# One transformer-like layer on one core: the order of every engine's instructions set by the kernel's own search instead of Tile's

## The chip, the cores and the metric

The kernel runs on one core of one Trainium2 chip. The metric is the device time of one execution in microseconds. Three executions of the kernel before took 917.09, 913.85 and 911.78 us; their median, 913.85 us, is the time before.

A core has a matrix engine (TensorE, PE in the profile, with its weight loads shown apart as PEld), a vector engine (VectorE, DVE), a scalar engine (ScalarE, ACT), GpSimd (POOL) and SyncE (SP), which issues most transfers. Each engine works through a list of instructions of its own in order, and waits on semaphores for the others. So the order of that list, which is fixed when the program is built, decides who waits for whom.

## What is computed

One layer of a hybrid backbone over 512 latent tokens and 256 context tokens with 1,024 channels, in float32. Cut to what matters:

```python
mod = silu(c) @ w_ada + b_ada                     # shifts, scales, gates
h, hc = rms_norm(x) * (1 + sc1) + sh1, rms_norm(ctx) * (1 + csc1) + csh1
aq, ak, av, dq, dk, dv, dz, da, db, ga, gd = split_cols(h @ w_in)   # the same for hc
y_attn = window_ctx_attention(q_a, k_a, v_a, k_ac, v_ac, attn_sink)
_, s_cf, s_cb = bidir_delta(context tokens, zero state)   # chunks of 64, both directions
o_dl, _, _ = bidir_delta(latent tokens, s_cf, s_cb)
y = sigmoid(ga) * (y_attn @ w_br_attn) + sigmoid(gd) * ((rms_norm(o_dl) * silu(dz)) @ w_br_dn)
x = x + gt1 * (y @ w_out)
x = x + gt2 * (square(relu((rms_norm(x) * (1 + sc2) + sh2) @ w_mlp1)) @ w_mlp2)
```

In the delta rule each chunk of 64 tokens needs the state that the chunk before it left:

```python
def step(S, xs):
    u = uv_c - w_c @ S
    o = qd_c @ S + intra_c @ u
    S = exp(gl_c) * S + k_tail_c.T @ u
```

There are 4 context chunks and 8 latent chunks in each direction. This is the serial part of the layer.

## The kernel before, in words

A matrix product in float32 is made of three products of float32r halves: weights and inputs are split into a rounded upper part (ScalarE copy) and the remainder (VectorE subtraction), and `mm3` (L293, L294, L295), `br_a` (L1086), `gate_tiles` (L1040) and `Pair.prod` (L1509) multiply upper by upper, upper by lower and lower by upper. `wload` brings a weight tile of 128x1024 into a ring of two raw buffers (`wr`), copies the upper part into one of three `wh` (L271) and makes the lower part in one of three `wl` (L276 on VectorE, or L273 on ScalarE and an accumulating transfer on GpSimd's queue, L274).

The stages, in the order in which the code is written and with the profile's times:

- 0 to 75 us: modulation vectors (`ada` L228, `columns` L244 to L258), the norm of x and ctx (L319 to L332), the modulated features (L299 to L301) and the first projections.
- 75 to 290 us: the other projections, queries and keys (`qk_norm` L451 to L465), the triangular matrices of the delta rule (`chunk_mats` L805 to L823) and their inversion on VectorE (`invert` L864, L865; transposes L841, L844, L875), attention (`scores` L545 to L582, `outputs` with its transposes L613 and products L602, L603). `weave` interleaves such pieces by hand.
- 290 to 393 us: the delta chain over the context chunks (`chain_step`: L1156 the products with the state, L1160 and L1161 on VectorE, L1175, L1181, L1187, L1195, L1206, L1213), the combination of the inverses (`combine` L885 to L909), the products within chunks (L786).
- 393 to 482 us: the chain over the latent chunks, both directions in turn, L1156 to L1223. Between its pieces `run_fill` puts matmuls of `br_a` and `gate_tiles` (L1040), which don't depend on the chain. `late_mod` (L1104, L1105) makes the remaining modulation vectors on VectorE, eight transfers and eight passes for each of four groups.
- 482 to 570 us: the norm of the chain's output (L1336), its transposes (L1341), the branch and output projections, the residual and the second norm.
- 570 us on: the MLP, one quarter with `mm3`, the others by a seven-product scheme (`Pair`, `combos`), and the products with the second MLP matrix (L1636 adds them).

SBUF is divided by the kernel itself: an arena hands out places when the code is traced, so that buffer addresses don't depend on the order of execution. What orders the instructions is Tile: the code is traced into one list, Tile finds the dependencies, and when the context ends, a scheduler with an estimate of each instruction's time lays out every engine's list, the earlier traced of those that it takes to be ready first. The kernel adds a few ties without semaphores: all functions of one activation table set stay behind its load (`act`, L154 to L168), and `follow` (L198) keeps one instruction behind another.

Of the kernel before, what the change touches and what calls it, by code (L numbers as in the profile page):

```python
# [2 lines left out]

# [14 lines left out]
NWR, NWS = 2, 3  # L18
# [13 lines left out]
FPAUSE, CPAUSE = 12, 12  # L32
NPL = ()
WEARLY = 0
ND1 = 3
NGD = 5
P = 128
# [8 lines left out]
HC = CH // 2  # L46
# [66 lines left out]
def tile_layer(ctx: ExitStack, tc: tile.TileContext, I: dict, out: bass.AP, dbg=None):  # L113
    nc = tc.nc
    V, A, G, PE = nc.vector, nc.scalar, nc.gpsimd, nc.tensor
# [17 lines left out]
    banks = Arena(lambda o, n: psum[:, o:o + n], 512, 8)  # L133
# [4 lines left out]
    alloc, bank = mem.get, lambda n=1: banks.get(n * 512)  # L138
# [13 lines left out]

    nosync = mybir.DependencyInfo(mybir.DependencyClass.NoSync, mybir.DependencyReason.DATA)
    actg = {"set": None, "head": None, "ops": []}  # L154

    def act(out_, in_, func, **kw):

        sets = TABLES.get(func)
        if sets and actg["set"] not in sets:
            head = A.preload_act_table_set(sets[0])  # L160
# [3 lines left out]
        r = A.activation(out_, in_, func, **kw)  # L164
        if sets:
            tc.add_manual_dep(r.ins, actg["head"].name, nosync, reason="table sets")
            actg["ops"].append(r.ins)
        return r  # L168

# [27 lines left out]

    def follow(later, earlier):  # L198

        tc.add_manual_dep(later.ins, earlier.ins.name, nosync, reason="order")  # L200

    def split(src, hi, lo, eng=None):
        A.activation(r32(hi), src, AF.Copy)  # L203
# [29 lines left out]
    last = [None]  # L233
# [159 lines left out]
    cost, sint = cs[:, :512], cs[:, 512:]  # L393
# [82 lines left out]
    own = [slice(0, 64), slice(64, 128)]  # L476
# [218 lines left out]
    t, t2 = alloc(TOK), alloc(TOK)  # L695
# [570 lines left out]
    for g in range(2):  # L1266
        ms = slice(16 * g, 16 * g + 16)
        f, b = xa[0][:, ms], xa[1][:, ms]
# [9 lines left out]
    for g in range(2):  # L1278
# [20 lines left out]
        for a in range(2):  # L1299
            lo, hi = quad(a, 0), quad(a, 1)  # L1300
# [37 lines left out]
    for qq in range(2):  # L1338
# [3 lines left out]
        for a in range(2):  # L1342
            n = 2 * qq + a
            t = alloc(512)
# [70 lines left out]
    ts = []  # L1415
# [13 lines left out]
    first = []  # L1429
# [5 lines left out]

    if WEARLY:
        load_first()
# [6 lines left out]
    for b in accs:  # L1444
        b.free()
    if not WEARLY:
        load_first()
# [139 lines left out]
    for hf in range(4):  # L1587
        act_, xs = [], []
        for f in range(0 if hf else FT):
            if first:  # L1590
                bufs, _, acc = first.pop(0)
            else:
                bufs = [alloc(1024), alloc(1024)]
                w = wload(I["wm1"][f], bufs=bufs)
                acc = bank()
                mm3(acc.ap.rearrange("p (n t) -> p n t", n=2), w, ms)
            r, hl = alloc(1024), alloc(1024)
            A.activation(r[:, :512], acc.ap, AF.Relu)
            acc.free()
            V.tensor_tensor(r[:, 512:], r[:, :512], r[:, :512], op=ALU.mult)  # L1600
            split(r[:, 512:], hl[:, :512], hl[:, 512:])
            for b in bufs + [r]:
                b.free()
            act_.append(hl)
            xs.append((r32(hl[:, :512]), r32(hl[:, 512:])))
            next(late)
        if hf == 0:
            xs7 = combos()
            for _ in late:
                pass  # L1610
            scr.free()
            for b in MH[0]:
                b.part(1024, 1024).free()
        w2 = lambda ct: wload(I["wm2"][ct * 4 + hf])
        ps_ = pairs[hf]
        for i, p_ in enumerate(ps_):
            p_.first()
            if i:
                p_.load2()
            if i + 1 < len(ps_):  # L1620
                p_.second()
            if i + 2 < len(ps_):
                ps_[i + 2].load1()
        ws = [w2(0), w2(1)]
        if hf:
            ps_[-1].second()
        accs = [bank(), bank()]
        ks = list(range(FT))
        for cols in (ks[:FT - 2], ks[FT - 2:]):
            for acc, w in zip(accs, ws):  # L1630
                mm3(acc.ap, w, [xs[k] for k in cols], start=(cols[0] == 0), stop=(cols[-1] == FT - 1), ks=cols)
        for ct in range(8):
            if ct > 1:
                accs.append(bank())
                mm3(accs[ct].ap, w2(ct), xs)
            V.scalar_tensor_tensor(xn_[ct], accs[ct].ap, modT[:, 3, ct:ct + 1], xn_[ct], op0=ALU.mult, op1=ALU.add)  # L1636
            accs[ct].free()
            if hf == 3:
                nc.sync.dma_start(out=out[ct], in_=xn_[ct])
            if hf < 3 and ct in (3, 5):  # L1640
                (pairs[hf + 1][0].load1 if ct == 3 else pairs[hf + 1][0].load2)()
        for b in act_:
            b.free()
        if hf < 3:
            pairs[hf + 1][1].load1()

# [109 lines left out]
```

## Time and profile before

| | |
|---|---|
| executions | 917.09, 913.85, 911.78 us |
| median | 913.85 us |
| span of the profiled execution, first to last instruction | 909.7 us |
| median less that span | 4.15 us |
| mean granted TensorE clock | 0.997 |
| bytes moved | 107.13 MB, 118 GB/s |

The profiled execution's time as a whole is not listed apart from its span; what lies around the span is part of the 4.15 us. In the rows below, a group's row has the line, the engine, the operation, output and inputs by name, the shapes and the count, then busy time and the mean of one in ns, then the idle time of the engine just ahead of these instructions and who ended it. A row of waits reads: who waited for whom, us in total, number of times, longest. A row of the timeline has start, duration, engine, line and operation. A row by stretch has start:end, length, and for PE, PEld, DVE, ACT and POOL the busy time and number of instructions, then the granted clock, the share of DMA time and GB/s. Matmul ends are modelled and overlap, so the distance between starts says more about TensorE than a matmul's duration: one 128x512 product of float32r starts 0.23 us after the one before it.

### The profile page before, as it was taken

Reading aid. Unit: us, or ns where it says so; the run is one execution under the profiler, and the core shown is the slowest. Engines: PE = TensorE matmul, PEld = TensorE weight load, DVE = VectorE, ACT = ScalarE, POOL = GpSimd, SP = SyncE. Lnnn points to the kernel's source line nnn. Section 1 sums busy time; section 2 is a strip of 40 time slices with the busy share of each in tenths; the row PEclk is TensorE's granted clock in tenths of the full one; section 3 lists DMA queues with packets and bytes.
Section 4 is the critical chain, followed back from the end, with each engine's and each line's share of the span. In section 5 each row is a group of like instructions: output and inputs, shape, how many; then the busy total and the mean of one; then the engine's idle time right before and its main releaser. Section 6 shows DMA issues by size and latency. Waiting matters only on the chain.

```text
span 909.7 us, 18033 instructions
## 1 busy us (share of the span) xinstructions
PE 873.9 (96%) x7564; PEld 721.3 (79%) x7564; DVE 652.9 (72%) x1111; ACT 496.9 (55%) x881; POOL 26.0 (3%) x42
## 2 busy tenths in 40 slices
PE   8999999989999998889999999999999999999998
PEld 6688667867777676656677789888898899889986
DVE  5665799876778999566666968896587567837631
ACT  6368764475768795475654434463265246424520
POOL 0000001010000001100000000000000000000000
PEclk9999999999999999999999999999999999999999
DMA  9824455532311136523143645453412332334031
GB/s 355 312 76 117 94 131 107 113 73 47 57 36 35 59 121 235 182 67 99 49 152 107 241 127 186 155 170 115 139 48 93 116 116 70 116 93 139 1 116 46
DMA packets 31985, 107.13 MB, mean 118 GB/s; under 512 B 4000, under 2 KB 4512, under 8 KB 31904
## 3 DMA queue, kind: packets, MB, share of 16 engines
q1 hardware_dynamic: 29600, 97.59, 32.1%
q0 software_dynamic: 2304, 8.39, 5.8%
q8 instruction: 59, 0.97, 0.4%
q14 instruction: 22, 0.18, 0.1%
HBM read 103.87 MB, written 2.10 MB: 116 GB/s over the span
## 4 chain that ended last, share of the span: by engine, by line
PE 60%; DVE 20%; ACT 11%; DMA 6%; issue 3%; SPq 0%; ACTq 0%; DVEq 0%
PE banks L293 12%; PE banks L294 12%; PE banks L295 12%; PE banks L1509 11%; PE banks L1040 5%; DMA m<-in_wada 3%; ACT m L164 2%; DVE m L865 2%; DVE m L864 2%; DVE m L1105 2%; DVE m L204 2%; DMA m<-in_wm 1%; DVE wl L276 1%; ACT m L928 1%; DVE m L875 1%
## 5 line engine op out<-in xcount | busy, mean ns | idle before, releaser
L293 PE MATMUL banks<-m,wh 128*128 128x512 f32 (+1 forms) x568 | 213.2, 376 | 0.5 <-ACT m L203 0.5
L294 PE MATMUL banks<-m,wh 128*128 128x512 f32 (+1 forms) x568 | 210.7, 371 | 0.3 <-DVE m L204 0.2
L295 PE MATMUL banks<-m,wl 128*128 128x512 f32 (+1 forms) x568 | 209.8, 370 | 0.0
L271 ACT ACTIVATE wh<-wr 128x1024 fp32r<-128x1024 f32 (+1 forms) x92 | 90.6, 987 | 130.5 <-PE banks L294 102.5
L1509 PE MATMUL banks<-m,m 128*128 128x256 f32 x1008 | 123.2, 284 | 0.9 <-ACT m L203 0.6
L1509 PEld LDWEIGHTS banks<-m,m 128*128 128x128 f32 x1008 | 121.9, 192 | 2.4 <-ACT m L203 1.2
L203 ACT ACTIVATE m<-m 128x512 fp32r<-128x512 f32 (+2 forms) x118 | 81.9, 719 | 75.0 <-DVE m L1487 12.0
L293 PEld LDWEIGHTS banks<-m,wh 128*128 128x128 f32 x568 | 107.0, 189 | 19.2 <-ACT m L203 1.0
L294 PEld LDWEIGHTS banks<-m,wh 128*128 128x128 f32 x568 | 107.0, 188 | 18.8 <-DVE m L204 1.2
L295 PEld LDWEIGHTS banks<-m,wl 128*128 128x128 f32 x568 | 106.9, 188 | 18.6 <-issue 0.7
L1040 PE MATMUL banks<-m,wh 128*128 128x512 f32 x320 | 108.2, 409 | 3.5 <-ACT m L164 3.5
L204 DVE TENSOR_TENSOR m<-m,m 128x512 fp32r<-128x512 f32 (+2 forms) x118 | 92.3, 804 | 22.3 <-ACT m L203 14.1
L276 DVE TENSOR_TENSOR wl<-wr,wh 128x1024 fp32r<-128x1024 f32 (+1 forms) x76 | 84.2, 1110 | 14.9 <-ACT wh L271 12.6
L1636 DVE SCALAR_TENSOR_TENSOR m<-banks,modT,m 128x512 f32<-128x512 f32 x32 | 24.0, 750 | 68.6 <-PE banks L295 68.4
L1040 PEld LDWEIGHTS banks<-m,wh 128*128 128x128 f32 x320 | 59.6, 190 | 16.5 <-ACT m L164 4.0
L1040 PE MATMUL banks<-m,wl 128*128 128x512 f32 x160 | 65.5, 410 | 0.0
L1105 DVE SCALAR_TENSOR_TENSOR m<-m,m 128x1024 f32<-128x1024 f32 x32 | 38.8, 1220 | 14.3 <-DMA m<-in_wada 14.2
L293 PE MATMUL banks<-m,m 128*128 128x256 f32 (+1 forms) x136 | 44.9, 344 | 1.4 <-ACT m L300 1.2
L294 PE MATMUL banks<-m,m 128*128 128x256 f32 (+1 forms) x136 | 45.1, 340 | 0.9 <-DVE m L301 0.8
L295 PE MATMUL banks<-m,m 128*128 128x256 f32 (+1 forms) x136 | 44.6, 337 | 0.0
L164 ACT ACTIVATE m<-banks,st 128x512 f32<-128x512 f32 (+1 forms) x32 | 23.5, 738 | 24.7 <-DVE st L570 24.4
L1040 PEld LDWEIGHTS banks<-m,wl 128*128 128x128 f32 x160 | 30.5, 190 | 6.5
(258 smaller groups left out, 1339.5 us busy)
## 6 DMA issues: line engine op xcount, KB each, us to landing
m<-in_wada SPq DMA_DIRECT2D x48, 512.0 KB, 5.3
wr<-in_wm SPq DMA_DIRECT2D x40, 512.0 KB, 3.6
wr<-in_win SPq DMA_DIRECT2D x39, 512.0 KB, 3.7
m<-in_wm SPq DMA_DIRECT2D x24, 512.0 KB, 3.9
wl<-in_win POOLq DMA_DIRECT2D x16, 512.0 KB, 5.6
m<-in_xT SPq DMA_DIRECT2D x8, 512.0 KB, 5.6
wr<-in_wbr SPq DMA_DIRECT2D x16, 256.0 KB, 2.6
wr<-in_wout SPq DMA_DIRECT2D x8, 512.0 KB, 3.8
```

What stands on the lines that cost most here:

```text
L164: r = A.activation(out_, in_, func, **kw)
L203: A.activation(r32(hi), src, AF.Copy)
L204: (eng or V).tensor_tensor(r32(lo), src, hi, op=ALU.subtract)
L271: upper[0] = A.activation(r32(hi), raw, AF.Copy)
L276: V.tensor_tensor(r32(lo), raw, hi, op=ALU.subtract)
L293: PE.matmul(acc, w[0][:, k, :], xhi, start=(start and i == 0), stop=False)
L294: PE.matmul(acc, w[0][:, k, :], xlo, start=False, stop=False)
L295: r = PE.matmul(acc, w[1][:, k, :], xhi, start=False, stop=(stop and i == n - 1))
L1040: PE.matmul(acc.ap, w[x][:, k, :], hx[k][y], start=(k == p == 0), stop=(k == KT - 1 and p == 2))
L1105: V.scalar_tensor_tensor(wa.ap, wa.ap, 0.5, scr.ap, op0=ALU.mult, op1=ALU.mult, accum_out=modT[:, grp, j:j + 1])
L1509: PE.matmul(dst, r32(self.w[w][i][:, k * P:(k + 1) * P]), xs7[x][k][j], start=(n == 0), stop=(n == 11))
L1636: V.scalar_tensor_tensor(xn_[ct], accs[ct].ap, modT[:, 3, ct:ct + 1], xn_[ct], op0=ALU.mult, op1=ALU.add)
```

## The change

The traced program stays the same; every instruction exists before and after with the same operands. `tie` records the kernel's own ordering ties. When tracing is done, `arrange` builds from the instructions a graph of its own (`needs`: reads and writes of cells of SBUF and banks of PSUM, rings of weight buffers, arena places that follow each other, the ties) and goes through it in time: of the instructions that are ready on the engine that is free first, the one traced first is taken, its occupancy and its end come from `Step.cost`, a transfer's end from a queue model, and what depends on it becomes ready `SIGNAL` = 120 ns later. Each engine's list is then tied in that order, so that Tile's scheduler has no choice left.

```diff
+SIGNAL = 120
...
+    ties = []
+
+    def tie(later, name):
+        tc.add_manual_dep(later, name, nosync, reason="order")
+        ties.append((later.name, name))
...
-                tc.add_manual_dep(head.ins, o.name, nosync, reason="table sets")
+                tie(head.ins, o.name)
...
-        tc.add_manual_dep(later.ins, earlier.ins.name, nosync, reason="order")
+        tie(later.ins, earlier.ins.name)
...
+    return ties
+
+
+class Step:
+
+    RINGS = {"wr": NWR, "wh": NWS, "wl": NWS, "st": 4}
...
+    def cost(self):
+
+        n = self.cols
+        if self.kind == "InstMatmult":
+            if self.dtype.endswith("32r"):
+                return max(60, 7 + .43 * n if n < 512 else 226), 300
+            if self.dtype.endswith("16"):
+                return 60, 200
+            if self.tile == (P, P):
+                return max(60, 110 if n <= P else 1.68 * n), 400
+            return (142 if self.tile[0] == P else 42 if self.tile[1] > HC else 20), 250
+        if self.kind == "InstStreamTranspose":
+            return 2010, 2100
+        if self.eng == "DVE":
+            own = 67 + 1.04 * n + 60 * self.psum if n > 8 else 100
+            return own, own + 85
+        if self.eng == "Activation":
+            own = 1290 if "Load" in self.kind else max(195, 36 + .893 * n) + 20 * self.psum
+            return own, own + 130
+        return 550, 560
+
+
+def needs(steps, ties):
...
+def arrange(tc, nc, ties):
+
+    steps = [Step(i) for i in nc.cur_bb.bb.instructions if "Boundary" not in type(i).__name__]
+    before = needs(steps, ties)
...
+    for _ in steps:
+        t, e = min((free[e] if here[e] else max(free[e], coming[e][0][0]), e) for e in engines if here[e] or coming[e])
+        while coming[e] and coming[e][0][0] <= t:
+            heapq.heappush(here[e], heapq.heappop(coming[e])[1])
+        k = heapq.heappop(here[e])
+        s = steps[k]
+        if "DMA" in s.kind:
+            rate, lag = (400., 1000) if e == "SP" else (159., 900)
+            links[e] = max(t + lag, links[e]) + s.bytes / rate
+            own, end = (350 if e == "SP" else 900), links[e] + 1300
+        else:
+            own, end = s.cost()
+            end += t
+        free[e] = t + own
+        own_ = "DMA" not in s.kind
+
+        def seen(n):
+            same = own_ and n < len(steps) and steps[n].eng == e
+            return free[e] if same and e == "PE" else end + 20 if same else end + SIGNAL
+
+        release(after[k], seen)
+        if e in last:
+            tc.add_manual_dep(s.ins, last[e], order, reason="order")
+        last[e] = s.name
...
-        tile_layer(tc, aps, out)
+        arrange(tc, nc, tile_layer(tc, aps, out))
```

More of the change, by code (lines that the diff above doesn't have):

```diff
@@ L1 @@
+import heapq
 import numpy as np
@@ L165, in act @@
         if sets:
-            tc.add_manual_dep(r.ins, actg["head"].name, nosync, reason="table sets")
+            tie(r.ins, actg["head"].name)
             actg["ops"].append(r.ins)
@@ new lines, in arrange, with release @@
+def arrange(tc, nc, ties):
+    steps = [Step(i) for i in nc.cur_bb.bb.instructions if "Boundary" not in type(i).__name__]
+    before = needs(steps, ties)
+    after, left, ready = [[] for _ in before], [len(b) for b in before], [0.] * len(before)
+    for k, b in enumerate(before):
+        for p in b:
+            after[p].append(k)
+    engines = {"PE", "DVE", "Activation", "Pool", "SP"}
+    free, links = dict.fromkeys(engines, 0.), {"SP": 0., "Pool": 0.}
+    coming, here, last = {e: [] for e in engines}, {e: [] for e in engines}, {}
+    def release(ns, at_):
+        for n in ns:
+            ready[n] = max(ready[n], at_(n))
+            left[n] -= 1
+            if not left[n]:
+                if n < len(steps):
+                    heapq.heappush(coming[steps[n].eng], (ready[n], n))
+                else:
+                    release(after[n], lambda _: ready[n])
+    first = [n for n, b in enumerate(before) if not b]
+    for n in first:
+        left[n] = 1
+    release(first, lambda _: 0.)
+    order = mybir.DependencyInfo(mybir.DependencyClass.NoSync, mybir.DependencyReason.DATA)
+    for _ in steps:
[8 more added lines that the diff above has]
+            own, end = (350 if e == "SP" else 900), links[e] + 1300
+        else:
+            own, end = s.cost()
[9 more added lines that the diff above has]
+        last[e] = s.name
```

76 lines of the change are left out of this document (added).

## The prediction

> **What bounds the kernel now.** I read the page's busy shares first, then the busy time by stretch, then who ends TensorE's idle time, then the timeline of the one stretch in which most of it lies.
>
> ```profile
> span 909.7 us, 18033 instructions
> ...
> PE 873.9 (96%) x7564; PEld 721.3 (79%) x7564; DVE 652.9 (72%) x1111; ACT 496.9 (55%) x881; POOL 26.0 (3%) x42
> ```
>
> TensorE is busy 873.9 of 909.7 us. The change alters no instruction, only the order, so it can win at most the 35.8 us in which TensorE stands, 3.9%. Where they lie is in the busy time by stretch (start:end, length, then the engines).
>
> ```profile
> 0.00:75.00 75.00, 70.92 (x480) 55.09 (x480) 45.61 (x90) 45.90 (x68) 2.69 (x7) 1.00 0.64 240
> 75.00:152.00 77.00, 72.52 (x737) 55.73 (x737) 66.53 (x126) 53.61 (x86) 6.04 (x7) 1.00 0.51 110
> 152.00:290.00 138.00, 132.64 (x999) 106.52 (x998) 106.83 (x192) 90.31 (x160) 8.97 (x12) 1.00 0.30 62
> 290.00:393.00 103.00, 93.96 (x1485) 71.57 (x1483) 85.99 (x154) 72.75 (x153) 7.26 (x14) 0.98 0.42 139
> 393.00:482.00 89.00, 82.27 (x1410) 59.25 (x1411) 60.73 (x130) 54.48 (x169) 1.04 (x2) 1.00 0.28 91
> 482.00:570.00 88.00, 87.25 (x485) 75.90 (x485) 65.79 (x107) 36.65 (x57) 0.00 (x0) 1.00 0.50 168
> 570.00:910.00 340.00, 334.29 (x1977) 297.23 (x1975) 221.43 (x316) 143.17 (x190) 0.00 (x0) 1.00 0.32 103
> ```
>
> Length less PE busy gives 4.1, 4.5, 5.4, 9.0, 6.7, 0.8 and 5.7 us (0.3 of the last lies behind the span). After 482 us the order has almost nothing left to win; about 26 us lie between 75 and 482 us. The waits on TensorE and, in the last two rows, on its weight loads (total us, times, longest) say for whom:
>
> ```profile
> PE banks L1040 <- ACT m L164: 3.5, 3, 2.3
> PE banks L1175 <- DVE m L1161: 3.3, 5, 0.9
> PE banks L896 <- issue: 2.0, 1, 2.0
> PE banks L810 <- DVE m L809: 1.7, 3, 0.9
> PE banks L1195 <- DVE m L1181: 1.7, 2, 1.2
> PE banks L503 <- ACT m L499: 1.5, 1, 1.5
> ...
> PEld banks L1175 <- DVE m L1161: 6.5, 12, 1.1
> PEld banks L1195 <- ACT m L1187: 5.4, 13, 1.7
> ```
>
> L1175 and L1195 are steps of the delta chain. While TensorE stands before them, the gate and branch matmuls of L1040, which depend on no chain step, are waiting later in its own queue. That is a wait an order can remove. The issue row (L896) isn't.
>
> **The change part by part.** Recording the ties, the step model and the search run while the program is built: no instruction, no transfer. Both programs have 5,857 matmuls, 1,074 VectorE, 849 ScalarE and 38 GpSimd instructions and 206 transfers on SP's queue. The separate wait instructions go from 58 to 49 on PE, 199 to 205 on DVE, 189 to 185 on ACT, 166 to 168 on SP, 34 to 35 on POOL: six fewer in all, and I cost them at nothing.
>
> What moves: 2,713 matmuls stand at another place in their queue, 706 VectorE, 476 ScalarE, 67 SP and 3 POOL instructions. Whether that helps depends on whether the price list that makes the new order is true, so I held it against the rows.
>
> ```profile
> L1105 DVE SCALAR_TENSOR_TENSOR m<-m,m 128x1024 f32<-128x1024 f32 x32 | 38.8, 1220 | 14.3 <-DMA m<-in_wada 14.2
> L1636 DVE SCALAR_TENSOR_TENSOR m<-banks,modT,m 128x512 f32<-128x512 f32 x32 | 24.0, 750 | 68.6 <-PE banks L295 68.4
> L203 ACT ACTIVATE m<-m 128x512 fp32r<-128x512 f32 x84 | 51.4, 625 | 57.6 <-DVE m L1487 12.0 <-DMA m<-in_wm 11.5 <-PE banks L1509 10.3
> L271 ACT ACTIVATE wh<-wr 128x1024 fp32r<-128x1024 f32 x76 | 80.5, 1062 | 119.1 <-PE banks L294 102.5 <-PE banks L1040 7.7 <-DMA wr<-in_wm 5.9
> ...
> wr<-in_wm SPq DMA_DIRECT2D x40, 512.0 KB, 3.6
> ...
> wl<-in_win POOLq DMA_DIRECT2D x16, 512.0 KB, 5.6
> ```
>
> The list gives 67+1.04*1024+85 = 1,217 ns for the first row (1,220), 67+1.04*512+60+85 = 744 for the second (750), 36+0.893*512+130 = 623 for the third (625), 1,080 for the fourth (1,062), 1,000+524,288/400+1,300 ns = 3.6 us for the fifth and 5.5 us for the last. All are within 2%. So an order that is free of waits by this list should be nearly so on the chip.
>
> *0 to 75 us.* TensorE's order is the old one up to 18 us, and 3.2 of the 4.1 us lie there:
>
> ```profile
> 0.00:18.00 18.00, 14.80 (x99) 12.72 (x99) 8.10 (x19) 11.60 (x15) 0.21 (x4) 1.00 0.89 339
> ```
>
> On SP five constants (ident, bones, selq, mi, nmask, 212 KB) move 10 to 13 places ahead, past w_ada loads. By the 400 bytes per ns of the list each load behind them is 0.5 us later; the same bytes are then missing later. The identb cast (L386) moves 33 places ahead on DVE, with its load, and would hold the modulations (L299, L301) behind it if that load were late. I take 0, bounds -0.5 (those bytes missing later) and +2 (the idle time of this stretch half as long again).
>
> *75 to 152 us.* Ahead of the three L810 waits and the L503 wait the new order puts independent matmuls of 1.1, 3.4, 1.6 and 0.5 us (the products moved ahead, at 0.23 us each, the distance of two L1040 starts in the last fence of this part). One L454 wait gets 0.45 us less ahead of it than before. VectorE is busy 66.5 of 77 us here and can itself be the limit. I take -1.5, bounds 0 and -3.
>
> *152 to 290 us.* Ahead of four waits of the transposes (L613) for the softmax and one of L895 come 0.5 to 2.5 us of other products. -2, bounds 0 and -3.7.
>
> *290 to 393 us.* From 300 to 350 us TensorE's order is unchanged. The two long L1040 waits on ScalarE's tanh (3.5 us) get chain steps put ahead of them: all 32 L1156 matmuls of the first latent step now stand together before them, where 11 of them stood behind, and before the second wait its 16 L1175 as well. The tanh also passes the weight copy (1.06 us) that it queued behind. The issue waits stay. -2.5, bounds 0 and -4.
>
> *393 to 482 us, the chain.* Ahead of nearly each L1175, L1195 and L1156 that waits, 11 to 49 more L1040 matmuls have gone by. Those are gone at the end: in the old order 43 of them lie between the last L1213 and the first transpose L1341, in the new one 24. 19*0.23 = 4.4 us of cover are lost there. What needs covering is this:
>
> ```profile
> 469.10 0.69 PE L1213 MATMUL banks<-m,m 64*64 64x64 f32 x32
> 469.72 0.50 PE L1040 MATMUL banks<-m,wl 128*128 128x512 f32 x1
> ...
> 480.73 1.09 PE L1341 MATMUL banks<-c_ident,m 128*128 128x128 f32 x8 [0.96 <-DVE m L1336]
> ```
> ```profile
> 469.70 0.42 DVE L1220 TENSOR_TENSOR m<-m,banks 128x256 f32<-128x256 f32 x1 [2.86 <-PE banks L1213]
> 470.94 1.23 DVE L1105 SCALAR_TENSOR_TENSOR m<-m,m 128x1024 f32<-128x1024 f32 x1 [0.82 <-DMA m<-in_wada]
> ...
> 472.09 1.22 DVE L276 TENSOR_TENSOR wl<-wr,wh 128x1024 fp32r<-128x1024 f32 x1
> 473.23 0.42 DVE L1221 TENSOR_TENSOR m<-m,m 128x256 f32<-128x256 f32 x1
> ...
> 478.31 1.22 DVE L1105 SCALAR_TENSOR_TENSOR m<-m,m 128x1024 f32<-128x1024 f32 x1
> ...
> 479.45 2.36 DVE L1336 TENSOR_TENSOR m<-m,oss 128x1024 f32<-128x1024 f32 x2
> ```
> ```profile
> 476.80 1.28 ACT L160 ACT_TABLE_LOAD   x1
> ```
>
> From the end of the chain to L1341 are 11.0 us. VectorE spends them on four L1105 passes, two weight splits (L276) and 0.8 us of waiting for a load, among the six instructions of the chain's tail. The new order is 1220, 1221, 1220, 1223, 1221, 1105, 1223, 1105, 1336: two passes (2*1.15, start to start) and both splits (2*1.13) and the wait leave the tail, 5.4 us. The table load, with a tanh, moves up 14 places on ACT, ahead of the last step's L1185 and L1187: what it saves in the tail it can cost there, and I count 0. So the tail is 11.0-5.4 = 5.6 us against 24*0.23 = 5.5 us of cover: the wait at L1341 stays what it was. Of the 6.7 us I count -5, bounds 0 (all given back at L1341) and -6.5.
>
> *482 us and on:* -0.5 (the one wait at 520 us gets seven matmuls ahead) and -0.5, bounds +1.5 and -2: nothing to win, and a few matmuls at 565, 575 and 677 us are moved ahead of what they need.
>
> *What it adds.* TensorE changes 366 times between kinds of matmul instead of 348. One change costs:
>
> ```profile
> 455.85 0.39 PE L1040 MATMUL banks<-m,wl 128*128 128x512 f32 x1
> 456.08 0.39 PE L1040 MATMUL banks<-m,wh 128*128 128x512 f32 x1
> 456.40 0.69 PE L1175 MATMUL banks<-m,m 64*64 64x64 f32 x32
> 457.02 0.50 PE L1040 MATMUL banks<-m,wh 128*128 128x512 f32 x1
> 457.36 0.39 PE L1040 MATMUL banks<-m,wl 128*128 128x512 f32 x1
> ```
>
> L1040 to the small group 0.32 us, and the first L1040 after it 0.34, where two L1040 in a row (the first two rows) are 0.23 us apart: 0.1 us a change, 18*0.1 = +1.8. [...] For waits that the new order makes itself I add +1, bounds 0 and +13 (the slower rival).
>
> The sum: 0-1.5-2-2.5-5-0.5-0.5+1.8+1 = -9.2 us, a span of 900.5. The runs shown are 911.8 to 917.1, median 913.85, 4.15 us over the profiled span, which includes what lies around it. 900.5+4.15 = 904.6 us.
>
> **The rivals.**
> *Slower: the splits stand at the head of VectorE's queue.* In the chain five weight splits (L276) move 13 to 29 places ahead on DVE. Each needs ScalarE's copy (L271), which needs a buffer that an L1040 product frees:
>
> ```profile
> ACT wh L271 <- PE banks L1040: 15.8, 6, 5.8
> ```
>
> Six such waits took 15.8 us on ScalarE, 2.6 each, on an engine that is 55% busy. If TensorE runs behind the list, the same wait stands on VectorE ahead of L1160, L1161 and L1181 of both directions: 5*2.6 = 13 us of chain, which the fixed stock of L1040 can't cover a second time. With nothing won in the chain: 913.85-9.2+5+13 = 922.6. It decides from about 9 us of such waits. Against it: the products that free the buffers are moved ahead as well, and the prices are true.
> *The waits move and the time stays.* The chain's 5 us come back at L1341 if the tail does not shrink, and half of the 6 us won before it is taken by VectorE, which has 66.5 of 77 us of work there: -9.2+5+3 = -1.2, 912.6. For it: the stock of L1040 is fixed. That the order on the chip isn't the one searched is no rival: the new queues differ as counted.
> *More than forecast.* Every wait that has independent work put ahead of it goes, the ends of the bounds from 75 to 482 us: -3-3.7-4-6.5+1.8 = -15.4, 898.4.
>
> **How the numbers follow.** Forecast 0.50 (898 to 910), more than forecast 0.12, waits move 0.20, slower 0.18. A difference under 0.5% (4.6 us) can't be told from none: the runs shown lie 0.6% apart. Faster by more, under 909.3: 0.48 of the forecast's 0.50, 0.12, and 0.05 of the third, 0.65. Within: 0.17. Slower: 0.18. The range 893 to 919 leaves out 0.05 below and 0.15 above.
>
> **What will show it.** Right: matmul starts without pause from one chain step to the next, the waits L1175 <- DVE L1161 and L1195 <- ACT L1187 below half, PE idle in the chain stretch near 2 us, only two L1105 between L1220 and L1336, an L1341 wait near 1 us. Wrong: an L1341 wait of 4 us or more (given back), L276 <- ACT L271 waits of over 2 us in the chain with L1160 behind them (slower rival), or new waits of L293 on L300 before 60 us. The forecast is wrong if TensorE's idle time stays above 31 us.

## The result, and the profile after

The changed kernel takes 914.86 us (median of 20 executions, 911.82 to 918.94); the kernel before, on the same chips, takes 911.91 us (20 executions, 910.37 to 917.09). The ratio is 1.0032, with a 95% interval of 1.0019 to 1.0045: 3 us slower, which is certain to be no gain, and less than the 0.5% that the forecast counted as a change. The forecast was 904.6 us.

Every line of the changed kernel stands 8 lower than before (L1040 is now L1048, L1175 is L1183); in the experiments' kernels it is 9. The profiled execution of the changed kernel took 918.01 us, 3 us above the median of its kind, so what the trace shows is somewhat more than the executions as a whole. On the page of the changed kernel, span and busy time:

```profile
span 916.2 us, 18029 instructions
...
PE 881.1 (96%) x7564; PEld 730.5 (80%) x7564; DVE 652.0 (71%) x1111; ACT 498.8 (54%) x881; POOL 26.1 (3%) x42
```

TensorE stands for 35.1 us where it stood for 35.8, and it is busy for 7.2 us more with the same matmuls. So two questions: why the idle time did not shrink, and why the same work takes longer. Busy time by stretch (start:end, length, engines, then the granted clock, DMA share and GB/s):

```profile
0.00:75.00 75.00, 70.44 (x461) 53.57 (x462) 46.61 (x90) 42.78 (x64) 1.68 (x6) 0.95 0.63 233
75.00:152.00 77.00, 76.01 (x767) 60.42 (x766) 63.16 (x117) 56.49 (x91) 7.07 (x8) 1.00 0.52 117
152.00:290.00 138.00, 128.25 (x972) 105.29 (x971) 104.07 (x193) 87.03 (x155) 8.99 (x12) 0.98 0.28 60
290.00:393.00 103.00, 97.78 (x1462) 75.14 (x1462) 90.37 (x162) 72.37 (x152) 7.27 (x14) 0.97 0.44 142
393.00:482.00 89.00, 83.41 (x1433) 59.68 (x1432) 56.85 (x124) 58.21 (x174) 1.04 (x2) 0.92 0.28 90
482.00:570.00 88.00, 86.92 (x472) 74.98 (x471) 65.72 (x108) 36.40 (x57) 0.00 (x0) 1.00 0.50 168
570.00:917.00 347.00, 338.24 (x2009) 301.42 (x2008) 225.23 (x322) 145.51 (x192) 0.00 (x0) 1.00 0.30 101
```

Length less PE busy is now 4.6, 1.0, 9.8, 5.2, 5.6, 1.1 and 8.8 us (0.8 of the last lies behind the span), against 4.1, 4.5, 5.4, 9.0, 6.7, 0.8 and 5.7. Idle time fell, as forecast, by 3.5 us from 75 to 152 us and by 3.8 us from 290 to 393 us. It rose by 4.4 us from 152 to 290 us, where attention lies, and by about 2.6 us in the MLP, and it fell by only 1.1 us in the chain. The clock was 1.00 in all stretches but one before, and is below it in four now. TensorE's waits (total us, times, longest) have new names:

```profile
PE banks L904 <- issue: 4.0, 1, 4.0
PE banks L1517 <- ACT m L211: 3.2, 2, 2.5
PE banks L1183 <- DVE m L1169: 2.7, 3, 2.2
PE banks L621 <- ACT m L172: 2.2, 1, 2.2
PE banks L610 <- ACT m L211: 2.1, 2, 1.7
...
PE banks L1048 <- ACT m L172: 1.7, 2, 1.0
```

The waits of before at L810 (1.7 us) and L503 (1.5) are gone from the list, and L1040's 3.5 us are halved (L1048). In their place stand L1517, L621 and L610.

The loss of rate shows when one cuts windows along the clock. The granted clock falls to exactly half (below: the half clock) for whole multiples of 3.41 us, in five pieces that make 34.1 us (before: one piece of 3.41 us, at 345 us; over all executions, before has 9.8 us and the changed kernel 29.1):

```profile
20.00:26.80 6.80, 6.32 (x34) 2.94 (x26) 5.07 (x11) 2.80 (x5) 0.00 (x0) 0.50 1.02 330
197.50:200.90 3.40, 3.40 (x42) 2.74 (x29) 1.25 (x2) 3.33 (x5) 0.00 (x0) 0.50 0.00 0
221.40:224.80 3.40, 3.40 (x13) 2.77 (x11) 2.50 (x4) 1.46 (x3) 0.00 (x0) 0.50 0.46 86
364.70:371.50 6.80, 6.29 (x139) 4.76 (x138) 1.07 (x3) 3.87 (x9) 0.57 (x2) 0.50 0.40 131
467.10:480.70 13.60, 11.88 (x191) 9.25 (x187) 8.50 (x21) 7.50 (x24) 0.00 (x0) 0.50 0.47 166
```

Each piece begins within 3.4 us behind a wait or a starved stretch: L621's 2.2 us, L610's 1.7, L904's 4.0, L1183's 2.2 in the list above, and the start's waits for w_ada (L236, 1.7 in three). Not every wait has one behind it: after L1517's 2.5 us, at 854 us, the clock stayed full. In the timeline of the last piece (start, length; idle ahead in brackets) L1048 matmuls begin 0.42 us apart (477.80 to 478.22), and 0.23 us apart once the clock is back (481.25 to 481.48):

```profile
465.89 0.46 PE L1183 MATMUL banks<-m,m 64*64 64x64 f32 x16 [2.20 <-DVE m L1169]
...
477.80 0.63 PE L1048 MATMUL banks<-m,wl 128*128 128x512 f32 x1
478.22 1.05 PE L1048 MATMUL banks<-m,wh 128*128 128x512 f32 x2
...
481.25 0.39 PE L1048 MATMUL banks<-m,wl 128*128 128x512 f32 x1
481.48 0.62 PE L1048 MATMUL banks<-m,wh 128*128 128x512 f32 x2
```

To see where the time goes I use a **work curve**: for a time t in the trace of before, the matmuls begun by then, each weighed with its duration there (1.1 us at most), and the time at which another kernel had begun the same weight; the number is how many us it is behind (negative: ahead). One profiled execution each; the other columns are experiments told below. In the chain (the row at 430) the small matmuls weigh much and the curve jumps by 1 to 2 us from one group to the next, so there it is rough.

| t in before, us | changed | c6 | c10 | c12 | c9 |
|---|---|---|---|---|---|
| 30 | 3.6 | 1.0 | 1.5 | 2.3 | 2.2 |
| 110 | 3.1 | 0.6 | 1.0 | 1.8 | 1.6 |
| 150 | -1.5 | -3.8 | -3.5 | -2.7 | -2.9 |
| 180 | -1.6 | -3.9 | -3.6 | -2.8 | -3.0 |
| 230 | 4.0 | -2.3 | -2.1 | -1.3 | 2.5 |
| 340 | 3.2 | -2.4 | -0.5 | -1.4 | 1.8 |
| 350 | -0.5 | -2.5 | -4.2 | -5.1 | -1.9 |
| 360 | 3.8 | -2.5 | 0.5 | -1.4 | 2.0 |
| 430 | -1.3 | -1.0 | -6.6 | -6.1 | -4.1 |
| 490 | 3.5 | -0.8 | -2.8 | -1.4 | 8.7 |
| 660 | 3.8 | -1.5 | -2.4 | -0.9 | 9.2 |
| 840 | 4.7 | -1.6 | -1.4 | -1.9 | 10.1 |
| 860 | 6.7 | -1.5 | 2.0 | -1.6 | 12.0 |

The changed kernel gains 4.6 us between 110 and 150 us and loses 5.6 between 180 and 230; it gains 3.7 at 340 to 350 and loses 4.3 in the next ten; it gains some 4 to 5 between 360 and 430 and loses as much by 490; and it loses 2.9 in two places of the MLP. Nearly every gain is followed by a loss.

### The profile page after: what moved, and what is told of

Its sections match the earlier page's. It is cut to its first block, busy times and chain, and to the rows that moved or that the text cites. A ratio compares the mean times of both kernels' runs of the same rounds, so it can differ in the third digit from the quotient of the medians.

```text
span 916.2 us, 18029 instructions
## 1 busy us (share of the span) xinstructions
PE 881.1 (96%) x7564; PEld 730.5 (80%) x7564; DVE 652.0 (71%) x1111; ACT 498.8 (54%) x881; POOL 26.1 (3%) x42
## 4 chain that ended last, share of the span: by engine, by line
PE 82%; ACT 6%; DVE 6%; DMA 3%; issue 2%; SPq 0%; DVEq 0%; ACTq 0%
PE banks L302 14%; PE banks L301 14%; PE banks L303 14%; PE banks L1517 12%; PE banks L1048 10%; PE banks L1094 3%; PE banks L621 2%; DMA m<-in_wada 1%; PE banks L1164 1%; PE banks L684 1%; ACT m L172 1%; DVE m L212 1%; PE banks L236 1%; PE banks L1203 1%; ACT m L211 1%
## 5 line engine op out<-in xcount | busy, mean ns | idle before, releaser
L1517 PE MATMUL banks<-m,m 128*128 128x256 f32 x1008 | 123.1, 283 | 3.9 <-ACT m L211 3.2
L1517 PEld LDWEIGHTS banks<-m,m 128*128 128x128 f32 x1008 | 122.0, 191 | 5.2 <-ACT m L211 3.6
L1048 PE MATMUL banks<-m,wh 128*128 128x512 f32 x320 | 109.2, 416 | 2.4 <-ACT m L172 1.7
L284 DVE TENSOR_TENSOR wl<-wr,wh 128x1024 fp32r<-128x1024 f32 (+1 forms) x76 | 84.3, 1110 | 13.0 <-ACT wh L279 10.6
L1048 PEld LDWEIGHTS banks<-m,wh 128*128 128x128 f32 x320 | 60.0, 193 | 15.7 <-ACT m L172 2.1
L1048 PE MATMUL banks<-m,wl 128*128 128x512 f32 x160 | 66.1, 414 | 0.0
L302 PE MATMUL banks<-m,m 128*128 128x256 f32 (+1 forms) x136 | 47.1, 348 | 0.7 <-DVE m L309 0.7
L301 PE MATMUL banks<-m,m 128*128 128x512 f32 (+1 forms) x136 | 45.4, 345 | 1.0 <-ACT m L308 1.0
L303 PE MATMUL banks<-m,m 128*128 128x256 f32 (+1 forms) x136 | 45.7, 339 | 0.0
L1048 PEld LDWEIGHTS banks<-m,wl 128*128 128x128 f32 x160 | 30.8, 193 | 7.0
L577 DVE TENSOR_REDUCE st<-banks 128x1 f32<-128x640 f32 (+1 forms) x24 | 22.9, 956 | 14.6 <-PE banks L553 12.2
```

The lines of the kernel that those rows point to most:

```text
L284: V.tensor_tensor(r32(lo), raw, hi, op=ALU.subtract)
L301: PE.matmul(acc, w[0][:, k, :], xhi, start=(start and i == 0), stop=False)
L302: PE.matmul(acc, w[0][:, k, :], xlo, start=False, stop=False)
L303: r = PE.matmul(acc, w[1][:, k, :], xhi, start=False, stop=(stop and i == n - 1))
L1048: PE.matmul(acc.ap, w[x][:, k, :], hx[k][y], start=(k == p == 0), stop=(k == KT - 1 and p == 2))
L1517: PE.matmul(dst, r32(self.w[w][i][:, k * P:(k + 1) * P]), xs7[x][k][j], start=(n == 0), stop=(n == 11))
```

## The experiments

But for m1 and the matmuls added in c5 and c8, the experiments have the instructions of the two kernels, and only the order that is tied differs. In place of the search stands the order itself, a list of step numbers:

```diff
-    for _ in steps:
-        t, e = min((free[e] if here[e] else max(free[e], coming[e][0][0]), e) for e in engines if here[e] or coming[e])
...
+    at, last = np.cumsum(np.frombuffer(zlib.decompress(base64.b85decode(ORDER)), np.int16).astype(int)), {}
+    for k in at:
+        s = steps[k]
+        if s.eng in last:
+            tc.add_manual_dep(s.ins, last[s.eng], order, reason="order")
+        last[s.eng] = s.name
```

A list that takes one kernel's order and, in a stretch of time, the other's, is made by sorting the steps of that stretch by their place in the other order; what stands in the stretch stays in it.

**c1: the ties alone.** The list is the order of before, on every engine.

> The order of the kernel before, on every engine, written down as a list and fixed with the change's own ties (no planner at all). Theory T (the change's ties cost nothing by themselves; the order gains some 10 us of waits and gives them back as TensorE time at half the granted clock, 34.1 us at 0.5 against 3.4 before): the same as before, 911.9 within 1 us, granted clock near 0.997. Rival R1 (what was lost is the price of fixing the order at all, through waits or semaphores that the ties add): 914 to 916.

Measured: 913.87 us, ratio to before 1.0014 (0.9998 to 1.0029). That lies between the two forecasts: tying a whole order costs between nothing and 2.6 us. The work curve stays within 0.7 us of before up to 360 us, and is about 3 us behind at 430 us, with two pieces of half clock (at 372 and 396 us; mean clock 0.994 against 0.997) that the profiled execution of before does not have, though the order is the same. A price of the ties of 1 or 2 us is thus not excluded. But c6 and c12 below carry the same ties and are faster than before, so what differs among the tied kernels is their order.

**c2: three stretches of the new order, cut by eye.** `sorted(steps of the stretch, key=place in the changed kernel)` for 105 to 155, 235 to 352 and 375 to 435 us.

> The order of before everywhere but in three stretches (105 to 155, 235 to 352 and 375 to 435 us of the trace of before), where the instructions of the stretch stand in the changed kernel's order. Theory T: in these stretches the changed kernel's work curve gains 4.4, 4.4 and up to 4.9 us on that of before (the third less, as filler from behind 435 us is not pulled in), and the light stretches with the half clock are left out: 899 to 904, granted clock 0.99 or more. Rival R2 (a wait that the order removes only comes back at the next joint, so stretches gain nothing of their own): 910 to 914.

Measured: 914.71 us, ratio 1.0018 (1.0005 to 1.0031). A miss: 4.4 us were won between 110 and 150 us, and 7.3 lost at once at 183 us, where the order of before should have run as ever, to a wait of 3.9 us for an exponential on ScalarE and 6.8 us of half clock behind it (128x512 products 0.43 us apart up to 189.2 us, 0.23 from 189.6). At 155 us the two orders had done the same work on TensorE, but not on VectorE, which was 3 us behind there while TensorE was 2 us ahead. Later cuts were laid where all five engines agree.

**c3: the chain as before.** The changed kernel's order, with 398 to 486 us in the order of before.

> The changed kernel's order, but the instructions of 398 to 486 us (the chain of 64x64 groups with L1048 between them) in the order of before, so that the large L1048 matmuls stand spread over the chain and do not run out ahead of its end. Theory T: the half clock at 466 to 480 us goes, the mean granted clock rises from 0.981 to 0.987 or more, and the 4.7 us that the changed kernel loses on before between 400 and 480 us are not lost: 909 to 911.5. Rival R3 (the half clock at the chain's end is beside the path, the chain sets the end there anyway): 914 to 916 with the clock up.

Measured: 914.40 us, ratio 1.0024 (1.0008 to 1.0040); the granted clock rose to 0.988 on average (0.984 in the changed kernel). The half clock at the chain's end went, and the time stayed: R3's result.

**c5 and c8: work put into the waits.** The changed kernel's order, with matmuls of ones that nobody reads added ahead of the matmuls that wait (`warm` holds them by the step that they run ahead of):

```diff
+        for i, e in [(i, "PE") for i in warm.get(k, ())] + [(steps[k].ins, steps[k].eng)]:
+            if e in last:
+                tc.add_manual_dep(i, last[e], order, reason="order")
```

> The changed kernel's order unchanged, with 64 matmuls added (128x128x128 of ones into a bank that nobody reads then) ahead of the matmuls that wait at 17 to 21, 193 to 196, 219 and 466 to 475 us, so that these waits hold TensorE work. Theory T2 (after the first three runs: over single executions the span rises by 0.3 us for each us at half clock, so the changed kernel's 20 us more of half clock cost it about 6 us, and its order is worth only 2 to 3 us at equal clock): granted clock up from 0.985 to 0.992 or more, and the median falls by 3 to 5 us to 910 to 912. The first theory T (the clock alone took back all the gain): 902 to 907. Rival R3 (the clock is incidental, the waits alone cost): the added work only delays what waits, 914.9 to 920, whatever the clock does.

(c4, a first form of c5 with three groups of the added matmuls written one place earlier and forecast at 902 to 907 us, gave no time: its queues would have waited for each other without end.) c5 measured: 918.25 us, ratio 1.0071 (1.0046 to 1.0096), clock 0.9935 on average. One added matmul took 0.27 us, where 0.11 us had been counted, so 64 of them overfilled the waits. With 25:

> The changed kernel's order with 25 added 128x128x128 matmuls instead of 64, since one took 0.27 us and not the 0.11 us they were counted with: 5 in the waits at 17 to 21 us, 8 at 193 to 196, 5 at 219, 7 at 466, so that no wait is overfilled. Theory T2 (0.3 us of span for each us at half clock): granted clock 0.990 or more instead of 0.985, median 911 to 913. Rival R3 (the clock is incidental): 914.9 to 917 whatever the clock does.

Measured: 914.59 us, ratio 1.0020 (1.0005 to 1.0035), clock 0.989. There is a third less half clock than in the changed kernel (19.5 us on average against 29.1) and 0.3 us less time (1.1 by the two ratios, each good to 1.4 us), where T2 forecast 2 to 4 us. Since the added work itself can delay, this does not settle what the half clock costs. It shows that filling these waits with idle work wins nothing that can be told from noise.

**m1: what holds the clock.** A kernel of its own; after each stretch of plain 128x512 matmuls comes one of another kind:

```diff
+    for n in (6, 4, 3, 2, 1):
+        for _ in range(24 // n + 8):
+            turned(n)          # n 128x512 matmuls, then ScalarE empties the bank and writes the next operand
+        full(60)
+    small(800)                 # 64x64x64
...
+    small(1600, 32, 4)         # 32x32x32
```

> None of the reference is computed; the output is zeros. TensorE alone runs stretches of 10 to 30 us, each behind 14 us or more of 128x128x512 matmuls back to back: first 6, 4, 3, 2 and 1 such matmuls per turn through an ACT eviction, then 64x64x64 groups back to back, then 32 and 16 of them with one 128x512 matmul between, then 32x32x32 back to back, then 128x128x128 back to back. Theory T: what holds the full clock is the share of the array that multiplies, not the time that TensorE is busy: the 64x64 and 32x32 stretches fall to half clock though nothing waits in them, the 128x512 matmuls hold it down to about half of the time busy. Rival R4 (time busy decides, so only waits bring the half clock): the 64x64 and 32x32 stretches stay at full clock and only the stretches with 1 or 2 matmuls per turn fall.

Busy time and clock in windows inside four of the stretches (three 128x512 matmuls per turn, one per turn, 64x64, 32x32; columns as above):

```profile
118.70:139.20 20.50, 11.55 (x36) 5.83 (x36) 0.00 (x0) 7.16 (x12) 0.00 (x0) 1.00 0.00 0
214.30:248.40 34.10, 18.31 (x24) 6.58 (x23) 0.00 (x0) 13.73 (x23) 0.00 (x0) 0.50 0.00 0
272.00:306.00 34.00, 20.33 (x1255) 18.98 (x1248) 0.00 (x0) 0.00 (x0) 0.00 (x0) 1.00 0.02 5
433.00:508.00 75.00, 32.20 (x2688) 29.65 (x2688) 0.00 (x0) 0.00 (x0) 0.00 (x0) 0.50 0.02 5
```

Six 128x512 matmuls per 3.41 us (36 in 20.5) held the full clock in this stretch, two or three (24 in 34.1) did not; the stretch with two per turn, three or four per 3.41 us (32 in 30.7), had a mean clock of 0.56. The 64x64 row held it (1.00), the 32x32 row did not (0.50), though TensorE waits for no other engine in either: over all of m1, issue ended 18.5 of the 19.0 us of idle time ahead of 64x64 matmuls and all 49.3 ahead of 32x32 ones. That 128x512 matmuls hold the clock down to about half of the time busy, as T had it, is not shown: with one per turn TensorE was busy for 54% of the time at a clock of 0.50. T's forecast was wrong on the 64x64 row and R4's on the 32x32 row. R4's reason, the time busy, is not excluded: the rows that held are busy for 56% and 60% of the time, the others for 54% and 43%, both at half clock, and these shares rest on modelled ends. So whether the size of a tile counts by itself stays open. The two small rows also went at nearly one pace: 34.0 us for 1,255 records and 75.0 for 2,688, 27 and 28 ns a record, two records for one float32 matmul.

**c6: the gain alone.** The order of before, with 90.5 to 181.5 us in the changed kernel's; at both ends the two orders have done the same work on all engines to 0.3 us.

> The order of before on every engine, except that the instructions of 90.5 to 181.5 us of its trace stand in the changed kernel's order; both ends lie where the two orders have done the same work on all engines to 0.3 us. Theory T2 (the order has a gain of its own of about 5 us in this stretch, given back by waits and half clock in other places): 906 to 908.5. Rival R2 (a wait taken away only comes back at the next joint): 911 to 913.

Measured: 910.33 us, ratio 0.9975 (0.9958 to 0.9993), between the two forecasts. It is faster than before, though by 2.3 to 2.5 us and not 5. Of the 4.4 us won by 150 us the curve loses 1.6 between 180 and 230 us, behind the joint, and 1.5 between 360 and 390, where its order is that of before; between 342 and 397 us the clock fell to half three times, as in c1 (mean clock of c6's profiled execution 0.992; in that of before, with 0.997, once). The gain is real and partly kept; R2 is wrong in its strong form.

**c7, c10 and c12: the losses alone.** The changed kernel's order, with places of loss in the order of before: 182 to 238 us (c10); that, 666 to 698 and 818 to 874 us (c12); those three and 384 to 494 us, the chain (c7).

> The changed kernel's order, but the instructions of 182 to 238 us of its trace (attention with the combine) in the order of before. Theory T2: the waits of 2.2 us at L621 and 1.7 us at L610 and the half clock behind each go, which are 5.0 us in the trace: 910 to 912 over many executions, granted clock up by 0.003 or more. Rival R2 (what is lost there only gives back the gain ahead of it, so it is lost in any order): 914 to 916.

> The changed kernel's order, but at the four places where its work curve falls behind that of before (182 to 238, 384 to 494, 666 to 698 and 818 to 874 us of its trace) the instructions stand in the order of before. Theory T2: the first place gives back 5.0, the second 1.6 as in the run with the chain alone, the others 1.4 and 1.9 us, in the trace's own terms, half clock included; over many executions some 5 to 8 us less than the changed kernel: 907 to 910, faster than both kernels. Rival R2 (the loss is not of these places, it follows from the gain ahead of them): 912 to 915.

> As the run with four places in the order of before, but the chain (384 to 494 us) stays in the changed kernel's order. Theory T2 (the chain's order with its light end costs some 10 us more at half clock, 0.3 us of span each): 911.5 to 913.5, granted clock lower than in that run. Rival R3 (the chain's order is worth nothing either way, and the clock at its end is beside the path): 909 to 910.5.

| kernel | us | ratio to before | half clock on average, us |
|---|---|---|---|
| changed | 914.86 | 1.0032 (1.0019 to 1.0045) | 29.1 |
| c10, attention back | 912.78 | 1.0009 (0.9993 to 1.0025) | 25.4 |
| c12, attention and MLP back | 908.65 | 0.9960 (0.9948 to 0.9972) | 23.0 |
| c7, the chain too | 909.79 | 0.9970 (0.9955 to 0.9986) | 10.6 |

(Half clock: twice one less the mean granted clock, times the span, averaged over the executions; before has 9.8.) Attention is worth 2.1 us, which lies between the two forecasts for c10, and the two MLP places 4.1. By the ratios, which take each kernel with before on its own chip, these are 2.1 and 4.5 us, good to about 2 us each, and 6.6 us together. c7 came out as T2 forecast. c12 is the fastest kernel of the study, 0.4% faster than before and a little below both of its forecasts. And T2 is wrong about the chain: c7 has 12.4 us less half clock than c12 and is no faster. The profile of c12 has the chain's wait and its half clock still in it, from the timeline and from the windows:

```profile
461.06 0.46 PE L1184 MATMUL banks<-m,m 64*64 64x64 f32 x16 [2.20 <-DVE m L1170]
```
```profile
393.00:482.00 89.00, 84.05 (x1356) 60.72 (x1355) 57.72 (x124) 54.86 (x167) 0.98 (x2) 0.92 0.28 91
```

**c9 and c11: the filler held back.** The 72 L1048 matmuls that the changed kernel runs from 430 to 461 us are spread evenly over 430 to 474 (c9); in c11 the three places of c12 are put back as well.

> The changed kernel's order, but its L1048 filler of 430 to 461 us (72 matmuls pulled ahead into the chain's early waits) is held back so that it stands evenly from 430 to 474 us; nothing else moves. Theory T2 (the filler ran out ahead of the chain's end; the light end then fell to half clock): the half clock at 466 to 480 us goes, and 3 to 5 us come back: 910 to 912. Rival R3 (the chain's latency sets the end, with or without filler): 914 to 916.

> Both: 182 to 238, 666 to 698 and 818 to 874 us in the order of before, and in the chain the changed kernel's order with its filler spread as in the other run. Theory T2 (the stretches add up, and the chain keeps the changed kernel's gain of 4 us at 384 to 400 us): 906 to 909, below the run with four places in the order of before (909.8). Rival R2: 909 to 912, no better than that run.

Measured: 923.32 us, ratio 1.0110 (1.0086 to 1.0133), and 917.24, ratio 1.0051 (1.0033 to 1.0069): both about 8.5 us worse than the same kernel with the filler early, and outside both of their forecasts. ScalarE's timeline of c9 shows part of the reason:

```profile
474.56 0.38 ACT L1194 ACTIVATE m<-banks 128x256 f32<-128x256 f32 x1 [1.06 <-PE banks L1184]
474.84 0.92 ACT L1196 ACTIVATE m<-banks,eg 128x64 f32<-128x64 f32 x4
475.62 1.11 ACT L173 ACTIVATE m<-banks 128x512 f32<-128x512 f32 x2
476.75 1.28 ACT L169 ACT_TABLE_LOAD   x1
478.04 1.06 ACT L280 ACTIVATE wh<-wr 128x1024 fp32r<-128x1024 f32 x1
479.01 0.36 ACT L1194 ACTIVATE m<-banks 128x256 f32<-128x256 f32 x1
```

The later filler's evictions, their table load and a weight copy now stand between the last two chain steps, and L1222 waits 3.6 us for L1196. The rest, some 5 us, came bit by bit from 430 to 474 us; which operation made them was not tried.

## Why the prediction was wrong, step by step

**"An order that is free of waits by this list should be nearly so on the chip."** This is the step that failed, and it failed at its condition: the order is not free of waits by the list. The search starts, at each moment, the earliest traced step among the ready ones; it does not hold an engine for a more urgent step that becomes ready a little later. Its own sums, followed through (no time of the chip), leave TensorE idle for 43 us in the new order, with large gaps at the very matmuls that wait on the chip: 2.6 us at the first L893 burst of attention (on the chip 0.7 there, 2.2 behind it), 2.2 at L610 (1.7), 1.7 at L611 (1.4), 2.3 at the chain's end, L1183 (2.2), 3.4 at L1517 (2.5). The same sums give the order of before 84 us of idle time, where the chip shows 35.8. So the search removed many short waits that the chip never had, and left long ones. The figures were in reach before the run; I compared the list with durations only. And the six rows compared were of VectorE, ScalarE and transfers. The list's prices for TensorE add up to 813 us, in either order, where TensorE is busy for 873.9 us before: L1040, for one, is counted with 108 us and takes 124 from start to start. By the sums TensorE is thus 7% too fast, which can make waits there that the chip does not have; how much of the 84 us this makes was not tried.

**152 to 290 us, -2.** The curve came out at +5.6 from 180 to 230 us, half clock included, and c10 gave back 2.1 us over many executions. The waits named at L613 (now L621) did not go, a longer one came: 2.2 us, where the order of before waits 1.2. VectorE and ScalarE of the changed kernel, ahead of it:

```profile
189.25 1.23 DVE L577 TENSOR_REDUCE st<-banks 128x2 f32<-128x1024 f32 x1
190.38 2.20 DVE L883 STREAM_TRANSPOSE m<-m 128x1024 f32<-128x1024 f32 x1
192.43 0.16 DVE L578 SCALAR_TENSOR_TENSOR st<-st,nsink 128x2 f32<-128x2 f32 x1
```
```profile
191.85 0.60 ACT L635 ACTIVATE m<-banks 64x512 f32<-64x512 f32 x1 [0.53 <-PE banks L611]
192.35 0.61 ACT L908 ACTIVATE m<-m 128x512 f32<-128x512 f32 x1
192.99 0.69 ACT L666 ACTIVATE m<-banks,c_prm 128x512 f32<-128x512 f32 x1
193.70 1.27 ACT L912 ACTIVATE m<-m 32x512 f32<-32x512 f32 x2
194.99 0.69 ACT L172 ACTIVATE m<-banks,st 128x512 f32<-128x512 f32 x1
```

The row maximum (L577) is done at 190.5 us. The 0.16 us that the softmax needs next (L578) stand behind a transpose of 2.2 us, and on ScalarE four groups of copies (L635 to L912) stand ahead of the exponentials (L172); L621 waits for those until 195.8 us. The order of before has L570 right behind L569 there:

```profile
191.25 1.21 DVE L569 TENSOR_REDUCE st<-banks 128x2 f32<-128x1024 f32 x1
192.49 0.16 DVE L570 SCALAR_TENSOR_TENSOR st<-st,nsink 128x2 f32<-128x2 f32 x1
```

This is the stall of the greedy rule: by the search's sums L578, which was traced before the transpose, is ready 0.1 us after VectorE comes free, and the search gives VectorE the transpose at that moment. A term of +1 for all "waits that the new order makes itself" was far too small: the three places measured 6.2 us (914.86 less 908.65).

**570 us and on, -0.5.** The curve loses 2.9 us, and c12 against c10 is worth 4.1. At 854 us L1517 waits 2.5 us (before 0.6) for the last of a row of weight splits on ScalarE and VectorE, and two 1.04 us copies, L1552 and L1553, stand ahead of that row:

```profile
848.64 1.04 ACT L1552 ACTIVATE m<-m 128x1024 f32<-128x1024 f32 x1
849.63 1.06 ACT L211 ACTIVATE m<-m 128x1024 fp32r<-128x1024 f32 x1
850.59 1.04 ACT L1553 ACTIVATE m<-m 128x1024 f32<-128x1024 f32 x1
851.54 1.56 ACT L211 ACTIVATE m<-m 128x512 fp32r<-128x512 f32 x2
```

**393 to 482 us, -5.** It came out near nothing. In the tail the order is as predicted (24 filler matmuls, two modulation passes), but it takes 7.2 us (477.3 to 484.4) and not 5.6; the wait at L1341, predicted to stay, is gone, covered by filler that ran at half clock up to 480.8 us. L1175's waits (3.3 us, 5 of them) became L1183's 2.7 in 3, of which one is 2.2, and idle time fell from 6.7 to 5.6, not to 2. The filler is a fixed stock, as the third rival said; it came back not at L1341 but ahead of it. In the traces, 134 L1040 matmuls lie between the chain's first latent L1175 and its last matmul before, and 168 in the changed kernel; the chain begins 3.5 us earlier (394.6 against 398.1 us) and ends 7.5 later (477.3 against 469.8). Between c7 and c12 no difference can be told (0.9 us by the ratios, good to 2), so neither way of running the chain is clearly better. The slower rival's mechanism (L276 waiting with L1160 behind it) is not what happened: among VectorE's waits of this stretch L276's, 2.4 us before, is gone.

**75 to 152 us, -1.5, bounds 0 and -3.** Right in sign and too small: the curve gains 4.6 us, the L810 and L503 waits are gone, and in c6 2.3 to 2.5 us of it reach the end of the kernel.

**290 to 393 us, -2.5.** Idle time fell by 3.8 us, L1040's waits as named among it. The time did not fall: behind the gain at 350 us stands the issue wait of L904, 4.0 us (before 2.0 and 1.2), with 6.8 us of half clock. I had said that these waits stay.

**0 to 75 us, 0.** The changed kernel is 3.6 us behind at 30 us with 6.8 us of half clock. With the same order there, c12 is 2.3 us behind with 3.4 us of half clock, and c10 and c3 are 1.5 and 1.0 us behind with none. So about 1 us is the order's, within the bounds; the rest differs between executions of one order, as the half clock does.

**The clock, in no term.** The sum took TensorE's rate as given. Over 237 single executions of before, the changed kernel and the experiments, span rises by 0.31 us (standard error 0.02) for each us of half clock among executions of the same kernel; by that, 19.3 us more than before (29.1 less 9.8) would be about 6 us, twice the whole loss. But the kernels among themselves don't follow it: c7 has 12.4 us less half clock than c12 and is no faster, c8 has 9.6 less than the changed kernel and is 0.3 us faster. What the half clock costs apart from the waits ahead of it is left open. Of the -9.2 us, the part that was worth something is what c12 keeps, about -3.6 (908.65 against 912.27).

**1.8 us for changes of matmul kind** can't be told apart in any run. **The 4.15 us around the span** was mis-sized: what lies around the span is 1.8 us (918.01 less 916.2), and the rest came from the three executions of before, whose median lies above that of all 20 (913.85 against 911.91). A small slip: the separate wait instructions are four fewer in all, not six; the term was nothing either way.

## What to carry to other kernels

Before trusting an order that a search has made, read the idle time that the search itself leaves on the limiting engine, and put the same sums to the old order: if they see waits there that the trace does not have, the gain over them will not come on the chip. Hold the price list against the limiting engine first: its sum should be the busy time that the trace shows. A greedy list order should be judged stage by stage, and can be mixed with the old one where all engines stand at the same point: three short stretches put back made 0.3% slower into 0.4% faster. In c2 a wait of 3.9 us on TensorE came with a loss of 7.3 us, more than its length, but filling such waits with idle work won nothing that could be told (c8: 0.3 us).

## What the runs showed of the hardware that was not expected

The half clock comes in pieces of 3.41 us on one fixed grid: in the changed kernel the pieces begin 177.5, 201.4, 344.7 and 447.1 us behind the first one, 52, 59, 101 and 131 times 3.413 us, the length of one piece in the trace, to 0.1 us. The same wait has a piece beside it in one execution and not in another: behind the 2.5 us at L1517 the clock stayed full in the changed kernel's profile and fell for 3.41 us, at 849 us, in c10's. Executions of the changed kernel have mean clocks from 0.979 to 0.989. Whether this depends on where a wait lies on the grid is not shown. Small matmuls took 27 to 28 ns a record in the long rows of m1, while a burst of 128 records of 32x32 ran at 8.6 ns a record (1.1 us) when nothing like it had gone just before, and the next, begun 2.6 us after the first, stood for 4.0 us: the "issue" wait. The order of before has it as well (2.0 and 1.2 us), and so have c1 (1.8 and 2.3), c3 and c10 (4.2 each), c9 (3.6) and c11 (3.2 and 2.4). It is not fixed, though: in c2's trace there is none at this place, where they begin 4.2 to 6.9 us behind each other and the last three run in 1.1 us each (the first, L895, waits 3.5 us for VectorE instead). So an order that keeps such bursts further apart is a thing to try.
